# Layer A's dense products by Strassen's seven products over 1024 tokens, with combinations by way of DRAM

## The chip, the cores and the metric

The kernel runs on one core of a Trainium2 chip. The metric is the time of one execution on the device in microseconds (us). TensorE multiplies matrices into PSUM, VectorE (DVE) and ScalarE (ACT) work on PSUM and SBUF, GpSimd (POOL) on SBUF alone; transfers are issued by SyncE (SP) or by POOL, and all of them are carried out by the same 16 DMA engines.

## The reference

2048 tokens of 1024 features go through a layer A (gMLP), then a layer B (attention over a window of 128 tokens with shared keys and values), then a norm. The change touches layer A alone:

```python
def gmlp_mixer(h, w_in, ln_g, ln_b, ws, bs, w_out):     # h = rms_norm(x): 2048 x 1024
    z = h @ w_in                                        # 1024 -> 3 * 2048
    u, v, g = jnp.split(z, 3, axis=-1)
    v = layer_norm(v, ln_g, ln_b)
    v = v.reshape(b, nc, CHUNK, A_GROUPS, A_GROUP_DIM)  # 16 chunks of 128 tokens, 16 groups of 128
    wsm = jnp.where(causal[None], ws, jnp.zeros_like(ws))
    sv = jnp.einsum('gts,bcsgd->bctgd', wsm, v) + bs.T[:, :, None]
    y = u * sv * jax.nn.silu(g)
    return y @ w_out                                    # 2048 -> 1024; x is added to it
```

Everything is float32. The kernel makes a float32 product from three passes: each operand is split into a high part (rounded to the type fp32r) and a low part (the rest), and high x high, high x low and low x high are summed (`mm3`).

## The kernel before, in words

Layer A goes over four blocks of 512 tokens (`NB`, `TB`). For a block:
- `vphase` computes v with tokens on partitions: 4 groups of 512 columns, 4 chunks of tokens, 8 tiles of features: 384 products of 128 x 128 by 128 x 512 (three passes each counted). ACT copies v from PSUM, VectorE takes the statistics (`bn_stats`) and normalizes in place. v stays in SBUF.
- 16 times `proj` for u and `proj` for g (features on partitions, 24 products each: 768 in all), and `gate`: the small product of v with the causal weights, times u, times silu(g) (the last multiplication on POOL), and the split of the result by ACT (high) and VectorE (low).
- `outproj_a`: 8 output tiles of 48 products (384), x added, the result stored to DRAM (`hD`) with its sum of squares.

Weights are a stream: `order` is the list of tiles (1024 columns), `fetch` loads the next by SP's queue and splits it on ACT and VectorE (`split`, L112 and L113), and `weights` keeps three tiles ready (`LOOKAHEAD`); four buffers hold them. Work that fits between products is hung on a count of half pieces (12 products): `half` counts, `at` and `after` register it. In this way the norm of the next block (`stat_steps`, `xn_step`) and 18 jobs `prescale_job` run in layer A: a job loads a tile of layer B's weights, multiplies it by the norm's gain and splits it on ACT and POOL, and stores it to DRAM (`wbD`) through POOL's queue. At the start TensorE multiplies raw x by the weights of v (`FIRST_W`), and the norm is applied to the result. SBUF holds 39 general slots of 512 columns (`GEN_BUFS`).

The order of instructions on each engine is set by the framework's planner from the order of the program; waits are by semaphore, and each engine and queue works in order.

## Time and profile before

| | |
|---|---|
| runs | 2269.25, 2267.98, 2269.21 us; median 2269.21 |
| profiled execution, first to last instruction | 2266.6 us |
| its own time beside its span | the runs' median is 2.6 us above the span |
| TensorE busy / loads of its weights | 99% / 85% |
| VectorE / ScalarE / POOL busy | 55% / 39% / 27% |
| moved by DMA | 319.59 MB, mean 141 GB/s |
| last eviction of layer A begins at | 1471.4 us |

How to read the lines: a line of a group has the source line, the engine, the operation, what it writes and reads, the shape, the count, then the busy time in us and the mean of one in ns, then the idle time of the engine ahead of it and who ended it. A line of the timeline has the start and the duration in us. Matmuls are pipelined, so the distance between two starts, not the duration of one, is the price of a product. In slices a digit is the busy share of one fortieth of the span in tenths.

### The profile page before, as it was taken

Reading aid. Unit: us, or ns where it says so; the run is one execution under the profiler, and the core shown is the slowest. Engines: PE = TensorE matmul, PEld = TensorE weight load, DVE = VectorE, ACT = ScalarE, POOL = GpSimd, SP = SyncE. Lnnn points to the kernel's source line nnn. Section 1 sums busy time; section 2 is a strip of 40 time slices with the busy share of each in tenths; the row PEclk is TensorE's granted clock in tenths of the full one; section 3 lists DMA queues with packets and bytes.
Section 4 is the critical chain, followed back from the end, with each engine's and each line's share of the span. In section 5 each row is a group of like instructions: output and inputs, shape, how many; then the busy total and the mean of one; then the engine's idle time right before and its main releaser. Section 6 shows DMA issues by size and latency. Waiting matters only on the chain.

```text
span 2266.6 us, 31103 instructions
## 1 busy us (share of the span) xinstructions
PE 2239.9 (99%) x11868; PEld 1922.9 (85%) x11868; DVE 1240.9 (55%) x2145; ACT 889.2 (39%) x1781; POOL 619.3 (27%) x667
## 2 busy tenths in 40 slices
PE   8999999999999999999999999999999999999997
PEld 7888888888888888888888888899889889989987
DVE  6543553354453344345335335258957867895785
ACT  5323332323332322323222223135725744662573
POOL 2034322023532003311101111225513622551461
PEclk9999999999999999999999999999999999999999
DMA  6245453335455324325332224543364255336322
GB/s 214 85 154 189 163 204 126 100 120 176 151 202 178 105 93 149 122 92 177 121 107 89 89 93 149 179 174 114 101 219 155 94 195 186 112 121 235 120 94 93
DMA packets 90005, 319.59 MB, mean 141 GB/s; under 512 B 10625, under 2 KB 12929, under 8 KB 78081
## 3 DMA queue, kind: packets, MB, share of 16 engines
q1 hardware_dynamic: 71424, 204.35, 26.8%
q0 software_dynamic: 18432, 113.26, 14.5%
q8 instruction: 94, 1.54, 0.3%
q14 instruction: 55, 0.44, 0.1%
HBM read 280.86 MB, written 36.70 MB: 140 GB/s over the span
## 4 chain that ended last, share of the span: by engine, by line
PE 85%; DVE 6%; issue 3%; ACT 2%; DMA 2%; POOL 2%; POOLq 0%; SPq 0%; DVEq 0%; ACTq 0%
PE ps L116 26%; PE ps L117 26%; PE ps L118 25%; PE ps L375 2%; PE ps L641 2%; PE ps L588 1%; PE ps L619 1%; PE ps L589 1%; DVE w L113 1%; PE ps L560 1%; DVE x_lo L113 1%; DMA s<-h 1%; ACT w L112 1%; DMA s<-in_xT 1%; POOL s L381 0%
## 5 line engine op out<-in xcount | busy, mean ns | idle before, releaser
L113 DVE TENSOR_TENSOR w<-w_raw,w 128x1024 fp32r<-128x1024 f32 x288 | 378.4, 1314 | 369.5 <-ACT w L112 369.1
L116 PE MATMUL ps<-x_hi,w 128*128 128x512 f32 x1280 | 506.3, 396 | 0.0
L117 PE MATMUL ps<-x_lo,w 128*128 128x512 f32 x1280 | 499.0, 390 | 0.0
L118 PE MATMUL ps<-x_hi,w 128*128 128x512 f32 x1280 | 498.6, 390 | 0.0
L112 ACT CAST w<-w_raw 128x1024 fp32r<-128x1024 f32 x288 | 301.0, 1046 | 499.2 <-PE ps L118 375.8
L116 PE MATMUL ps<-w,x_hi 128*128 128x256 f32 (+1 forms) x1024 | 332.1, 324 | 0.0
L118 PE MATMUL ps<-w,x_lo 128*128 128x256 f32 (+1 forms) x1024 | 330.5, 323 | 0.0
L117 PE MATMUL ps<-w,x_hi 128*128 128x256 f32 (+1 forms) x1024 | 330.4, 323 | 0.0
L116 PE MATMUL ps<-s,w 128*128 128x512 f32 (+1 forms) x800 | 305.2, 383 | 4.5 <-ACT s L112 4.5
L117 PE MATMUL ps<-s,w 128*128 128x512 f32 (+1 forms) x800 | 305.0, 381 | 0.1
L118 PE MATMUL ps<-s,w 128*128 128x512 f32 (+1 forms) x800 | 304.4, 381 | 0.0
L118 PEld LDWEIGHTS ps<-x_hi,w 128*128 128x128 f32 x1280 | 240.3, 188 | 50.5
L116 PEld LDWEIGHTS ps<-x_hi,w 128*128 128x128 f32 x1280 | 240.7, 188 | 46.0
L117 PEld LDWEIGHTS ps<-x_lo,w 128*128 128x128 f32 x1280 | 240.8, 188 | 45.7
L627 POOL TENSOR_SCALAR_AFFINE_SELECT s<-s 128x512 fp32r<-128x512 f32 x256 | 184.8, 749 | 101.7 <-ACT s L621 69.3
L117 PEld LDWEIGHTS ps<-w,x_hi 128*128 128x128 f32 x1024 | 194.7, 190 | 15.6
L116 PEld LDWEIGHTS ps<-w,x_hi 128*128 128x128 f32 x1024 | 194.6, 190 | 15.5
L118 PEld LDWEIGHTS ps<-w,x_lo 128*128 128x128 f32 x1024 | 194.7, 190 | 15.1
L381 POOL TENSOR_TENSOR s<-s 128x512 f32<-128x512 f32 x64 | 82.2, 1284 | 396.0 <-DVE s L380 335.6
L116 PEld LDWEIGHTS ps<-s,w 128*128 128x128 f32 x800 | 150.2, 188 | 33.8 <-ACT s L112 6.0
L117 PEld LDWEIGHTS ps<-s,w 128*128 128x128 f32 x800 | 150.5, 188 | 29.2 <-DVE s L113 1.4
L118 PEld LDWEIGHTS ps<-s,w 128*128 128x128 f32 x800 | 150.4, 188 | 28.5
(145 smaller groups left out, 2871.5 us busy)
## 6 DMA issues: line engine op xcount, KB each, us to landing
w<-wb POOLq DMA_DIRECT2D x72, 1024.0 KB, 5.4
w_raw<-in_wug SPq DMA_DIRECT2D x128, 512.0 KB, 3.7
w_raw<-in_wv SPq DMA_DIRECT2D x64, 512.0 KB, 3.7
w_raw<-in_wao SPq DMA_DIRECT2D x64, 512.0 KB, 3.8
s<-in_xT SPq DMA_DIRECT2D x88, 256.0 KB, 4.4
wb<-phl POOLq DMA_DIRECT2D x18, 1024.0 KB, 5.2
w_raw<-in_wbo SPq DMA_DIRECT2D x32, 512.0 KB, 3.8
s<-h SPq DMA_DIRECT2D x64, 256.0 KB, 4.7
```

The source lines that it names most:

```text
L112: A.copy(hi, src)
L113: (lo_eng or V).tensor_tensor(lo, src, hi.bitcast(F32), ALU.subtract)
L116: PE.matmul(ps, ah, bh, start=first, stop=False)
L117: PE.matmul(ps, ah, bl, start=False, stop=False)
L118: PE.matmul(ps, al, bh, start=False, stop=last)
L375: PE.matmul(psm[:, t * P:(t + 1) * P], vt[t][j // 4][:, (j % 4) * P:(j % 4 + 1) * P], ws_sb[:, j, :], start=True, stop=True)
L381: last[0] = G.tensor_tensor(sv, sv, sg, ALU.mult).ins
L560: PE.transpose(pst[:, h * P:(h + 1) * P], sts[t2][:, h].rearrange("p s d -> p (s d)"), ident_r)
L588: PE.matmul(o, lq, kst[:, kv, 0, band, :], start=True, stop=False)
L589: PE.matmul(o, lq, kst[:, kv, 1, band, :], start=False, stop=True)
L627: G.affine_select(out=y.rearrange("p (h q) -> p h q", h=4), in_=x.rearrange("p (h q) -> p h q", h=4), pattern=[[0, 4], [sign, P]], base=ba ...
L641: PE.matmul(po[:, par * 256:(par + 1) * 256], w, x[:, par * 256:(par + 1) * 256], start=n == 0, stop=n == 3)
```

## The change

Layer A goes over two halves of 1024 tokens. Every dense product is seen as 2 x 2 blocks on each side (two halves of the contracted features; two halves of the tokens; two of the output columns, for u and g the columns of u and those of g) and done with seven products of blocks in the form of Winograd, in the order `STEPS`. `chain_of` runs the seven and combines their results: partial sums accumulate in PSUM, others are copied out by ACT (or added to the residual by VectorE) and added later by VectorE. A product of blocks has 4 feature tiles and 12 passes per bank.

- The input side. The seven combinations of x (`combos`: four additions) are split into high and low and stay in SBUF (`X`, 14 tiles of 2048 columns). For the first half VectorE makes them ahead of and during the first v stage (`start_block`, `third`, `fourth`); the norm of x is now applied before the products. For the second half POOL makes them during the first out stage (`x_steps`), the split goes to DRAM (`put_dram` with two buffers `hl`, `setD`), and `load_set` brings it back. The combinations of y take the same way (`ug_pair`, `finish_pair`), as two sets for the two halves of y's features.
- The weight side. `fetch_a` builds the four combined tiles of each weight set on POOL in the first half, from quarters loaded by SP, and stores them (`sumD`); in the second half they are loaded. A weight tile has 512 columns. LOOKAHEAD stays 3, so three tiles are three times 12 products.
- v goes to DRAM (`vD`) through POOL's queue and comes back by groups (`load_v`), and is normalized then (`mix`). The causal weights and their constants take the same way (`wscD`).
- The residual is loaded, and partial and final results of the out stage stored, through POOL's queue (`out_pair`, `pD`, `hD`).
- The prescale jobs are cut into 36 halves, 18 in each out stage.
- General slots: 19 in layer A, 39 in layer B from a pool of its own.

The core of the diff:

```diff
+STEPS = ("11", "12", "s2", "s1", "s3", "s4", "22")
...
+    def fetch_a(n, quarters, sums, make):
...
+        if si is None:
+            raw = rd(qr(n))
+        elif not make:
+            raw = rd(sums[si])
+        elif n == "s2":
+            r21, r22, raw = rd(qr("21")), rd(qr("22")), rd(qr("11"))
+            G.tensor_tensor(r21, r21, r22, ALU.add)
+            G.tensor_tensor(raw, r21, raw, ALU.subtract)
+            G.dma_start(sums[0], r21)
+            G.dma_start(sums[1], raw)
+            kept[key] = r21
...
+        w = wraw[0].tile([P, 1024], F32R, name="wa", bufs=W_BUFS)
+        split(w[:, :512], w[:, 512:], raw)
...
+        def load_set(key, n):
+            new_set(n)
+            for z in range(2):
+                G.dma_start(X[n][z].rearrange("p (k t) -> p k t", k=4), setD[key][n][:, :, z, :].bitcast(F32R))
+
+        def combos(q11, q12, q21, q22, eng):
+            yield q11
+            yield q21
+            t1 = slot()
+            eng.tensor_tensor(t1, q12, q11, ALU.subtract)
+            eng.tensor_tensor(q11, q22, t1, ALU.subtract)
+            yield q11
+            yield t1
+            eng.tensor_tensor(q12, q22, q12, ALU.subtract)
+            yield q12
+            yield q22
+            eng.tensor_tensor(q21, q21, q11, ALU.subtract)
+            yield q21
+
+        def put_dram(key, n, k, t):
+            hl = hltile()
+            split(hl[:, :TB], hl[:, TB:], t)
+            G.dma_start(setD[key][n][:, k], hl.rearrange("p (z t) -> p z t", z=2).bitcast(F32))
...
+        def chain_of(width, product, keep, done, on_step):
+            a = [bank() for _ in range(width)]
+            product(a, "11", True)
+            p1 = keep(a, 11)
+            on_step(0)
+            c = [bank() for _ in range(width)]
+            product(c, "12", True)
+            done(11, c, p1)
+            on_step(1)
+            product(a, "s2", False)
+            u2 = keep(a, 12)
+            on_step(2)
+            c = [bank() for _ in range(width)]
+            product(c, "s1", True)
+            p5 = keep(c, 22)
+            on_step(3)
+            product(a, "s3", False)
+            done(22, a, p5)
+            on_step(4)
+            product(c, "s4", False)
+            done(12, c, u2)
+            on_step(5)
+            product(a, "22", False)
+            done(21, a, None)
+            on_step(6)
...
+        def by_columns(banks, n, first):
+            xh, xl = X[n]
+            for ps in banks:
+                wh, wl = weights()
+                for k in range(4):
+                    cs, ts = slice(k * P, (k + 1) * P), slice(k * TB, (k + 1) * TB)
+                    mm3c(ps, wh[:, cs], wl[:, cs], xh[:, ts], xl[:, ts], first and k == 0)
+                half()
...
+        for sb in range(2):
+            ln = vphase(sb)
             pend = None
+            for kh in range(2):
+                for jj in range(4):
+                    pend = ug_pair(sb, kh, jj, ln, pend, ("Y0_", sb) if kh == 1 and jj == 3 else None)
+            acc = [None, None]
+            if sb == 0:
+                for k in range(4):
+                    for i, f in enumerate(x_steps(k)):
+                        after(4 + 8 * k + i, f)
+            for i in range(18):
+                after(6 + 2 * i, lambda i=i, sb=sb: prescale(18 * sb + i))
+            finish_pair(pend, ln)
+            for kh in range(2):
+                for m in range(2):
+                    nxt = None
+                    if m == 1:
+                        nxt = ("Y1_", sb) if kh == 0 else ("X", 1) if sb == 0 else None
...
+                    out_pair(sb, kh, m, acc, nxt)
```

More of the change, by code (lines that the diff above doesn't have):

```diff
@@ L107, in trunk @@
     g_sb = glob.tile([P, 4, KD], F32, name="g_sb")
[L108 removed]
+    nc.sync.dma_start(g_sb, gains)
     a_g, kv_g, b_g, f_g = (g_sb[:, i, :] for i in range(4))
@@ new lines, in xn, with put, second @@
+        def xn(h, k):
+            V.scalar_tensor_tensor(xq[h, k], xq[h, k], a_g[:, k:k + 1], rbox[h], ALU.mult, ALU.mult)
+        def put(n, k, t):
+            ks = slice(k * TB, (k + 1) * TB)
+            split(X[n][0][:, ks], X[n][1][:, ks], t)
+        start_block(0, 0, 0)
+        while events:
+            half()
+        for k in range(4):
+            xn(0, k)
+            put("11", k, xq[0, k])
+        h0 = now[0]
+        for k in range(4):
+            def second(k=k):
+                xn(0, k + 4)
+                put("12", k, xq[0, k + 4])
+            at(h0 + 1 + k // 2, second)
```

478 lines of the change are left out of this document (297 added, 181 removed).

## The prediction

> **What bounds the kernel now.** I read the page first (busy shares, slices, transfer rate), then the timeline of TensorE, then the groups of instructions by line, then short windows for the transfers.
>
> ```profile
> span 2266.6 us, 31103 instructions
> ...
> PE 2239.9 (99%) x11868; PEld 1922.9 (85%) x11868; DVE 1240.9 (55%) x2145; ACT 889.2 (39%) x1781; POOL 619.3 (27%) x667
> ...
> PE   8999999999999999999999999999999999999997
> ...
> DVE  6543553354453344345335335258957867895785
> ...
> POOL 2034322023532003311101111225513622551461
> ...
> GB/s 214 85 154 189 163 204 126 100 120 176 151 202 178 105 93 149 122 92 177 121 107 89 89 93 149 179 174 114 101 219 155 94 195 186 112 121 235 120 94 93
> ```
>
> TensorE never pauses; POOL and the transfers have room in every slice of layer A (slices 1 to 26). The timeline of TensorE gives the price of one product and shows that nothing stands between products:
>
> ```profile
> 6.76 1.22 PE L116 MATMUL ps<-w,s 128*128 128x512 f32 x2 [6.76 <-ACT w L112]
> ...
> 117.22 0.39 PE L118 MATMUL ps<-x_hi,w 128*128 128x512 f32 x1
> 117.45 1.05 PE L375 MATMUL ps<-ws_sb,s 128*128 128x128 f32 x8
> 118.25 0.48 PE L116 MATMUL ps<-x_hi,w 128*128 128x512 f32 x1
> ...
> 1439.64 0.39 PE L118 MATMUL ps<-s,w 128*128 128x512 f32 x1
> ...
> 1469.78 0.39 PE L116 MATMUL ps<-s,w 128*128 128x512 f32 x1
> ```
>
> From 1439.64 to 1469.78 lie 133 starts: 0.2266 us each. A gate's small products add about 0.9 us. Layer A of before has 4 blocks x (384 + 768 + 384) = 6144 wide products: 1392 us, with 64 gates at 0.9 (58 us), the first start at 6.8 and some small change to the last eviction of the layer, which begins at 1471.4 (row below). So layer A is TensorE's own rate, and layer B takes the remaining 795 us, unchanged in kind.
>
> ```profile
> L400 DVE TENSOR_TENSOR s<-ps,s x32: 682/692/692, 304.9 to 1471.4; 128x512 f32<-128x512 f32 x32
> ```
>
> **What the change removes.** Seven products for eight: 6144 x 7/8 = 5376, 768 fewer, 768 x 0.2266 = **-174 us** on TensorE, the full gain. Gates: 16 x 2 x 4 small products per 1024 tokens, as many as before. What it adds lies on the other engines and the queues; their prices:
>
> ```profile
> L381 POOL TENSOR_TENSOR s<-s 128x512 f32<-128x512 f32 x64 | 82.2, 1284 | 396.0 <-DVE s L380 335.6 <-issue 60.4
> ...
> L378 DVE SCALAR_TENSOR_TENSOR s<-ps,lngb_sb,cb 128x512 f32<-128x512 f32 x64 | 48.0, 750 | 176.6 <-PE ps L375 176.6
> ...
> L112 ACT CAST s<-s 128x512 fp32r<-128x512 f32 x75 | 46.6, 621 | 282.0 <-POOL s L381 257.3 <-POOL s L184 22.4 <-DVE s L184 2.3
> ...
> L113 DVE TENSOR_TENSOR s<-s 128x512 fp32r<-128x512 f32 x64 | 44.3, 693 | 149.5 <-ACT s L112 149.5
> ...
> L113 POOL TENSOR_TENSOR phl<-pw,phl 128x1024 fp32r<-128x1024 f32 x18 | 43.2, 2400 | 16.2 <-ACT phl L112 16.2
> ...
> L330 POOL TENSOR_TENSOR pw<-pw,g_sb 128x1024 f32<-128x1024 f32 x18 | 34.1, 1892 | 73.9 <-DMA pw<-in_wqg 65.7 <-DMA pw<-in_wkv 8.3
> ...
> L299 DVE SCALAR_TENSOR_TENSOR s<-s,g_sb 128x512 f32<-128x512 f32 x32 | 25.2, 816 | 15.2 <-DMA s<-in_xT 14.8 <-DVE s L299 0.3
> ...
> L401 POOL DMA_DIRECT2D h<-s x32 | 17.9, 558 | 248.4 <-DVE s L400 248.4
> ...
> L184 DVE TENSOR_TENSOR s<-s 128x512 f32<-128x512 f32 x24 | 16.6, 691 | 14.7 <-ACT s L181 14.7
> ...
> L196 POOL TENSOR_TENSOR r<-m,neghalf 128x4 f32<-128x4 f32 x11 | 11.4, 1037 | 54.3 <-DVE m L194 54.2
> ...
> L193 DVE TENSOR_REDUCE m<-s 128x4 f32<-128x512 f32 x11 | 7.5, 683 | 0.2
> ```
>
> So a 512-wide POOL operation costs 1.28 us, a transfer issued from POOL 0.56 us of POOL, a 512-wide VectorE operation 0.69 us. For the transfers, two windows in which they ran at a full share:
>
> ```profile
> core 0: us, PE busy (x) PEld busy (x) DVE busy (x) ACT busy (x) POOL busy (x), PEclk, DMA share, GB/s
> 4.00:8.00 4.00, 1.22 (x2) 0.50 (x2) 2.01 (x3) 1.76 (x2) 0.00 (x0) 1.00 0.99 387
> 8.00:12.00 4.00, 3.98 (x10) 2.88 (x11) 1.61 (x3) 2.05 (x3) 0.00 (x0) 1.00 1.04 406
> ```
>
> I take 390 GB/s as all that the transfers can move. Each half of the new layer A (1024 tokens) has three stages: v (56 weight tiles of 12 products, 152 us of TensorE), u and g (8 pairs of 168 products and four gates, 38.1 + 3.6 = 41.7 us each, 333 us), out (4 pairs, 152 us). I go stage by stage and add what each takes above TensorE's time.
>
> **Start: +33.** Before, TensorE began on raw x at 6.8. Now the first product needs the norm: 8 tiles of x and 3 of weights (2.9 MB at 390 GB/s from 2 us on, 9.4 us), then one after another square, add, split (ACT 0.62, POOL 1.28), mean, reduce, power (1.04), back through TensorE, multiply, split: about 12 us. First product at about 22: +15. The first four steps (11, 12, s2, s1) take TensorE 10.9 us each, and VectorE must have made s2 by 22 + 30 = 52: 16 scalings (13), 16 splits of x (11), 12 splits of weights (8), 8 square adds and a second norm (9), 8 combinations (6), 8 operations on the first quarter (6), 53 us from 21 on: s2 complete at 74 instead of 52, of which I take +18 (3 to 22, as TensorE works while the tiles come). Bounds of the term +20 to +45.
>
> **u and g, first half: +10.** A pair has two weight sets to build: per set 4 POOL adds and 4 stores of the sums. POOL per pair: 8 adds + 4 combinations of y + 4 gates = 16 x 1.28 = 20.5, and 8 + 7 + 4 transfers x 0.56 = 10.6: 31 of 41.7 us. VectorE: 14 + 7 splits, 4 x 0.75 gate, 4 multiplies, 6 evictions, 16 short scalings: about 28. Bytes: per set 10 reads and 4 writes of 0.262 MB, y 3.7 MB, v and its constants 1.3 MB: 12.3 MB, 32 us. All three fit, none by much, and the lookahead is three tiles of 2.7 us where it was three of 5.4. A wait of POOL for VectorE's split stands ahead of the weight sums on POOL's queue, and TensorE is three tiles away from these. Between 0 and +54 (second rival); I take +10, nearest to the bound in which the sums fit.
>
> **Out, first half: +138.** Here everything meets: 8 weight sets are built, residuals come and go through POOL's queue, half of the prescale jobs and all combinations of x for the second half are placed here, and Y1 and X are loaded. POOL: 32 weight adds, 20 combinations, 4 gates, 14 square adds, 2 norm splits: 72 x 1.28 = 92; 18 half prescale jobs at 0.95 + 1.20 = 39; transfers: 32 sums, 32 residual loads, 32 stores, 36 of prescale, 52 of x, 28 of sets, 9 others = 221 x 0.56 = 124. **Sum 255 us against 152 of TensorE.** Bytes: weights 29.4, residuals 16.8, prescale 14.2, x 21, two sets 29.4, y 3.7: 114 MB, at 390 GB/s **290 us**. TensorE needs the weight sums, the residuals and the sets, all of which stand in the same queue in about the order of the program, so it can run only a few tiles ahead. What covered such work before was POOL at 27%; that cover is gone here. I take the transfers' 290: 290 - 152 = +138. Bounds: if the prescale work alone slides into the next stage (39 + 36 x 0.56 = 59 of POOL's 255) +44; if handoffs of POOL and the two buffers of the split combinations cost a tenth more, 330, +178.
> The Trainium skill, DMA: Bandwidth & Descriptors, section Specifications, gives about 358 GB/s as the limit from HBM for one core. By it the stage would be 114/0.358 = 318 us and the sum 28 us more; the windows above moved 387 and 406, so here the trace disagrees and I stay with it.
>
> **v, second half: +3; u and g, second half: +2.** The sums are read, not made: POOL has 32 stores in the one, 8 operations and 11 issues (16.4 us) per pair in the other, VectorE as above without the x work. Up to +10 and +5, for the load of X and short of nothing below zero.
>
> **Out, second half: +22.** POOL: 8 + 14 + 2 operations (31), prescale 39, 121 issues (68): 138 of 152. Bytes: weights 14.7, residuals 16.8, prescale 14.2, Y1 14.7, the late part of Y0 some 10, the rest 6: 76 MB, 195 us; part of it runs in the last pair of u and g, so half of the 43 is taken (0 to +45).
>
> **Layer B: +2.** Same work; its slots now come free only when layer A's pool closes (0 to +10).
>
> **Sum:** -174 + 33 + 10 + 138 + 3 + 2 + 22 + 2 = **+36**. The profiled span is 2266.6, 2.6 us below the median 2269.2 of the runs; both move alike, so 2269 + 36 = **2305 us**.
>
> **Rivals.**
> 1. *POOL lets the late work go by* (ends faster). Place: the prescale jobs and stores of the first out stage, which nothing in layer A reads, slide into the second v stage, where POOL has 32 issues in 152 us; the transfers slide with them, and the sets of X stream into the v stage, whose steps last 10.9 us. Then the stage costs about +50 and the second out stage +15: -174 + 33 + 5 + 50 + 3 + 2 + 15 + 2 = -64, **2205**. It decides from 36 us of slid work on. For it: the row of slices shows POOL at 0 to 3 tenths where it has no due work. Against: the jobs stand earlier in the program than the sums that TensorE waits for.
> 2. *VectorE and POOL shut each other out* (slower still). In the prescale work of before:
>
> ```profile
> 537.34 1.23 DVE L113 TENSOR_TENSOR w<-w_raw,w 128x1024 fp32r<-128x1024 f32 x1 [1.73 <-ACT w L112]
> ...
> 541.91 2.40 POOL L113 TENSOR_TENSOR phl<-pw,phl 128x1024 fp32r<-128x1024 f32 x1 [1.16 <-ACT phl L112]
> ...
> 542.82 2.58 DVE L113 TENSOR_TENSOR w<-w_raw,w 128x1024 fp32r<-128x1024 f32 x1
> ```
> The same split takes VectorE 1.23 us at 537.34 and 2.58 at 542.82, where it ends 1.09 us after POOL's operation (541.91 + 2.40): it waited for it. If every such pair excludes the other, POOL's chain in a u/g pair becomes 20.5 + 10.6 and 25 VectorE operations with two inputs in SBUF x 0.69 (17.2) = 48.3 against 41.7: 8 x 6.6 = +53 instead of +10; in the out stage 255 + 107 x 0.69 = 329 instead of 290, 39 more: **2387**. For it: the three rows. Against: it needs each one to be hit. The Trainium skill, SBUF — State Buffer, section Who interferes with whom, states the same: a VectorE instruction with two SBUF inputs contends with a GpSimd one that reads SBUF, and the second blocks; the rows agree.
> 3. *All of it is hidden*: issues from POOL turn out to cost TensorE nothing and only the start remains: -174 + 33 + 6 = -135, **2134**. Against: 255 us of POOL in a stage of 152.
> 4. *The products don't fall*: excluded by the count, 5376 for 6144; TensorE's records of layer A would show it.
>
> **How the numbers follow.** Forecast 0.50 (own range 2250 to 2370), rival 1 0.27, rival 2 0.13, rival 3 0.10. Faster: rivals 1 and 3 and the lowest edge of the forecast, 0.39; within 0.2% (4.5 us, what a measurement of this kernel can tell) 0.04; slower 0.57. Range 2180 to 2400: it leaves out rival 3 and the upper part of rival 2.
>
> **What would show it.** In the profile after: first product at about 22 us; TensorE's slices at 9 in u/g and v, and at 4 to 6 for a stretch of some 290 us that begins near 550 us; in it POOL at 8 or 9 tenths and over 350 GB/s; waits of TensorE for weight splits that wait for POOL or for a transfer. Wrong would be: no such stretch (rivals 1 and 3), or one already from 200 us on (rival 2).

## The result, and the profile after

The changed kernel takes **2638.72 us** (median of four runs, 2633.39 to 2648.25) against 2269.06 for the kernel before (four runs, 2267.98 to 2269.25): ratio 1.1636, 95% interval 1.1613 to 1.1659. The forecast was 2305 with a range to 2400: the sign was right, the size was not; +370 us where +36 was forecast. The page of the changed kernel, in the order of the lines shown of before:

```profile
span 2631.7 us, 33230 instructions
...
PE 2202.0 (84%) x11100; PEld 1836.3 (70%) x11100; DVE 1645.3 (63%) x2847; ACT 972.6 (37%) x2151; POOL 1248.0 (47%) x1552
...
PE   4788988879553357899999996748899999999998
...
POOL 2675555665567577211344445554243253253352
PEclk8999999989776678899999998879999999999999
...
GB/s 164 227 257 230 214 233 229 230 218 300 332 269 299 337 257 340 201 172 144 178 198 210 203 319 311 295 270 244 134 113 184 163 111 184 175 100 183 188 94 88
```

TensorE's matmuls fell from 11868 to 11100, by 768: the products were saved as forecast. But TensorE's row, 9 from the second slice on before, now shows 3 to 8 in most of slices 1 to 16 and again in slices 25 to 27, and the granted clock falls with it. So the question is what each stage takes above its products. Its boundaries are read from TensorE's timeline, at the turn from the last products and gates of one stage to the first products of the next, to some 5 us; the windows between them (length; busy time and count of TensorE, its weight loads, VectorE, ScalarE, GpSimd; granted clock, share of the DMA engines, GB/s):

```profile
core 0: us, PE busy (x) PEld busy (x) DVE busy (x) ACT busy (x) POOL busy (x), PEclk, DMA share, GB/s
24.00:248.00 224.00, 182.07 (x690) 138.08 (x691) 148.23 (x230) 79.24 (x143) 127.81 (x169) 0.91 0.63 212
248.00:671.00 423.00, 363.68 (x1598) 293.94 (x1598) 294.81 (x405) 135.59 (x245) 247.35 (x269) 0.92 0.71 242
671.00:1046.00 375.00, 191.28 (x677) 144.68 (x676) 143.13 (x166) 71.71 (x122) 254.56 (x323) 0.73 0.88 301
1046.00:1218.00 172.00, 162.82 (x683) 129.99 (x682) 78.75 (x130) 54.88 (x93) 31.82 (x50) 0.96 0.58 189
1218.00:1562.00 344.00, 339.63 (x1592) 280.62 (x1590) 252.41 (x396) 135.15 (x243) 129.07 (x143) 1.00 0.62 207
1562.00:1823.00 261.00, 179.19 (x680) 141.08 (x681) 112.52 (x144) 57.97 (x98) 141.85 (x183) 0.82 0.88 291
1823.00:2632.00 809.00, 780.37 (x5184) 706.78 (x5182) 602.29 (x1357) 427.63 (x1192) 310.71 (x410) 0.99 0.42 144
```

In this order: v, u/g and out of the first half, the same of the second half, layer B. Above TensorE's need (152, 333, 152 us, by the prediction's working), and with the start at 24 us instead of 6.8:

| term | forecast | measured |
|---|---|---|
| start and v, first half | +33 | +89 (17 + 72) |
| u/g, first half | +10 | +90 |
| out, first half | +138 | +223 |
| v, second half | +3 | +20 |
| u/g, second half | +2 | +11 |
| out, second half | +22 | +109 |
| layer B | +2 | +12 (809 against 797 from the last product start of layer A) |
| products | -174 | -174 |

The terms add up to +380; 13 of it stood in layer A of before as well (its last product started at 1469.8, its products and gates make 1457), which leaves 367 for the 365 between the two spans.

Two bills of the prediction came out: GpSimd's busy time in the first out stage (forecast 255 us, row 254.56) and the bytes of the out stages (forecast 114 and 76 MB; 301 GB/s x 375 us = 113, 291 x 261 = 76). That the first agrees to the digit is luck: its parts were 92 us for 92 (additions and the like), 42 for 39 (prescale) and 133 for 124 (issues), and they overlap by 12. So the work was counted rightly; what failed is the time that this work takes, and where TensorE waits for it. The waits in the first out stage (engine, waiting instruction, releaser: us in all, times, longest):

```profile
PEld ps L126 <- ACT wa L116: 165.8, 15, 48.8
...
ACT hl L116 <- POOL s L439: 87.5, 12, 16.0
DVE hl L117 <- ACT hl L116: 86.2, 21, 13.8
DVE s L606 <- DMA s<-p: 49.7, 10, 14.3
...
POOL s L439 <- DMA s<-in_wqg: 31.5, 10, 9.9
```

TensorE waits for ScalarE's casts of the weights, and ScalarE is busy 72 of 375 us there. It waits itself: each engine takes its instructions in order, and at the head of ScalarE's queue stands the cast of a prescaled tile (made at L439), with weight casts behind it. GpSimd, which makes that tile, stands at its head for the tile's load. One such chain in the timelines of ScalarE, of GpSimd and of TensorE (start, duration; in brackets the idle time before and what ended it):

```profile
910.22 0.62 ACT L116 CAST hl<-s 128x512 fp32r<-128x512 f32 x1 [5.16 <-DMA wb<-hl]
926.28 0.62 ACT L116 CAST hl<-s 128x512 fp32r<-128x512 f32 x1 [15.44 <-POOL s L439]
927.50 0.62 ACT L116 CAST wa<-w_raw 128x512 fp32r<-128x512 f32 x1 [0.60 <-POOL w_raw L214]
```
```profile
912.40 0.55 POOL L437 DMA_DIRECT2D s<-in_wqg  x1
...
914.03 1.27 POOL L213 TENSOR_TENSOR w_raw<-w_raw 128x512 f32<-128x512 f32 x1
925.21 1.04 POOL L439 TENSOR_TENSOR s<-s,g_sb 128x512 f32<-128x512 f32 x1 [9.91 <-DMA s<-in_wqg]
926.20 1.27 POOL L214 TENSOR_TENSOR w_raw<-w_raw 128x512 f32<-128x512 f32 x1
```
```profile
928.17 0.80 PE L126 MATMUL ps<-xh,wa 128*128 128x512 f32 x1 [48.40 <-ACT wa L116]
...
933.06 0.63 PE L126 MATMUL ps<-xh,wa 128*128 128x512 f32 x1
933.49 0.63 PE L127 MATMUL ps<-xl,wa 128*128 128x512 f32 x1
...
938.17 0.39 PE L127 MATMUL ps<-xl,wa 128*128 128x512 f32 x1
938.40 0.39 PE L128 MATMUL ps<-xh,wa 128*128 128x512 f32 x1
```

GpSimd issues the load of a tile that nothing in layer A needs at 912.40, multiplies it at 925.21 and only then makes the weight sum of L214 (926.20); the cast of that sum follows at 927.50, the product at 928.17, after 48 us in which TensorE had nothing. In 34 of these 48 us ScalarE stood for prescale jobs: 13.57 ahead of its cast at 903.92, then 5.16 (for one of the two buffers of the split) and 15.44. And TensorE restarts slowly: products start 0.43 us apart until 933.9, 0.23 from 937.2 on.

### The profile page after: what moved, and what is told of

Same layout as the page of the kernel before. It is cut to its first block, busy times and chain, and to the rows that moved or that the text cites. A ratio compares the mean times of both kernels' runs of the same rounds, so it can differ in the third digit from the quotient of the medians.

```text
span 2631.7 us, 33230 instructions
## 1 busy us (share of the span) xinstructions
PE 2202.0 (84%) x11100; PEld 1836.3 (70%) x11100; DVE 1645.3 (63%) x2847; ACT 972.6 (37%) x2151; POOL 1248.0 (47%) x1552
## 4 chain that ended last, share of the span: by engine, by line
PE 43%; DMA 17%; POOL 11%; DVE 10%; issue 8%; ACT 2%; SPq 0%; POOLq 0%; DVEq 0%; ACTq 0%
PE ps L128 7%; PE ps L126 7%; PE ps L127 7%; PE ps L120 6%; PE ps L122 5%; PE ps L121 5%; DMA w_raw<-in_wug 3%; DMA s<-in_wqg 3%; DMA s<-in_xT 2%; DMA Y_s<-hl 2%; PE ps L909 1%; DMA s<-p 1%; DMA vp<-v 1%; DVE wa L117 1%; DVE vp L534 1%
## 5 line engine op out<-in xcount | busy, mean ns | idle before, releaser
L126 PE MATMUL ps<-xh,wa 128*128 128x512 f32 x1344 | 563.1, 419 | 270.1 <-ACT wa L116 180.8
L128 PE MATMUL ps<-xh,wa 128*128 128x512 f32 x1344 | 556.4, 414 | 50.7 <-DVE wa L117 50.5
L117 DVE TENSOR_TENSOR wa<-w_raw,wa 128x512 fp32r<-128x512 f32 x448 | 386.2, 875 | 292.4 <-ACT wa L116 291.4
L127 PE MATMUL ps<-xl,wa 128*128 128x512 f32 x1344 | 551.3, 410 | 0.0
L126 PEld LDWEIGHTS ps<-xh,wa 128*128 128x128 f32 x1344 | 269.8, 201 | 342.4 <-ACT wa L116 205.6
L116 ACT CAST wa<-w_raw 128x512 fp32r<-128x512 f32 x448 | 273.3, 619 | 401.5 <-PE ps L128 308.5
L128 PEld LDWEIGHTS ps<-xh,wa 128*128 128x128 f32 x1344 | 267.4, 199 | 127.6 <-DVE wa L117 65.8
L127 PEld LDWEIGHTS ps<-xl,wa 128*128 128x128 f32 x1344 | 269.4, 200 | 60.2
L126 PE MATMUL ps<-wa,xh 128*128 128x512 f32 x448 | 183.7, 412 | 17.8 <-ACT s L476 6.4
L127 PE MATMUL ps<-wa,xh 128*128 128x512 f32 x448 | 183.9, 411 | 4.7 <-DVE wa L117 4.7
L120 PE MATMUL ps<-w,hn 128*128 128x256 f32 x640 | 184.1, 288 | 0.0
L121 PE MATMUL ps<-w,hn 128*128 128x256 f32 x640 | 182.3, 285 | 0.0
L122 PE MATMUL ps<-w,hn 128*128 128x256 f32 x640 | 182.2, 285 | 0.0
L128 PE MATMUL ps<-wa,xl 128*128 128x512 f32 x448 | 181.9, 407 | 0.1
L534 DVE TENSOR_SCALAR vp<-vp,mv,rs 128x128 f32<-128x128 f32 x256 | 149.3, 655 | 14.5 <-DMA vp<-v 11.0
```

Source lines behind the costliest of these rows:

```text
L116: A.copy(hi, src)
L117: (lo_eng or V).tensor_tensor(lo, src, hi.bitcast(F32), ALU.subtract)
L120: PE.matmul(ps, ah, bh, start=first, stop=False)
L121: PE.matmul(ps, ah, bl, start=False, stop=False)
L122: PE.matmul(ps, al, bh, start=False, stop=last)
L126: PE.matmul(ps, ah, bh, start=first, stop=False, skip_group_check=True)
```

## The experiments

All are edits of the changed kernel; where not said otherwise each is one run with its profile. e2, e4, e5, e9, e10, e13 and e17 leave out part of the work, the others do all of it. The four runs of the changed kernel lie within 15 us of each other, and a stage that an edit leaves alone comes out within some 5 us (v of the first half takes 223 to 226 in e1, e4, e5 and e7, v of the second 170 to 175 in e8 to e13); smaller differences say nothing. Their stages in us (v, u/g, out of the first half; v, u/g, out of the second), from TensorE's timelines:

| kernel | time | v | u/g | out | v | u/g | out |
|---|---|---|---|---|---|---|---|
| changed kernel | 2638.7 | 224 | 423 | 375 | 172 | 345 | 261 |
| e1 prescale moved | 2539.9 | 225 | 421 | 298 | 171 | 396 | 192 |
| e2 no sums | 2481.1 | 192 | 346 | 329 | 175 | 342 | 259 |
| e3 issued later | 2582.8 | 228 | 414 | 364 | 170 | 342 | 231 |
| e4 quarter sets | 2528.5 | 223 | 413 | 336 | 159 | 338 | 225 |
| e5 = e1 + e4 | 2450.4 | 223 | 419 | 249 | 163 | 392 | 165 |
| e6 sums on VectorE | 2611.1 | 219 | 409 | 371 | 174 | 344 | 260 |
| e7 = e3 + prescale moved | 2505.7 | 226 | 412 | 297 | 201 | 344 | 190 |
| e8 longer lead | 2617.6 | 221 | 405 | 373 | 170 | 342 | 256 |
| e9 no stores of sums | 2585.6 | 219 | 404 | 357 | 170 | 344 | 254 |
| e10 no additions | 2581.2 | 206 | 395 | 367 | 173 | 346 | 259 |
| e11 nine raw buffers | 2639.7 | 224 | 431 | 376 | 170 | 344 | 260 |
| e12 casts on VectorE | 2646.3 | 229 | 417 | 385 | 170 | 349 | 262 |
| e13 loads only | 2489.5 | 193 | 352 | 336 | 175 | 343 | 256 |
| e14 gate and y on VectorE | 2617.6 | 231 | 410 | 376 | 169 | 335 | 263 |
| e15 gate on VectorE | 2623.9 | 233 | 414 | 377 | 170 | 335 | 259 |
| e16 = e7 + e14 | 2503.9 | 225 | 413 | 300 | 206 | 337 | 187 |
| e17 sums on VectorE, no stores | 2546.2 | 200 | 380 | 355 | 174 | 343 | 258 |
| e18 = e7 + e6 + later stores | 2509.6 | 219 | 409 | 300 | 210 | 343 | 191 |

**The out stages: bytes, or waits at the heads of the queues?** The theory of the prediction (T1: bytes; the rate was too high) stood against a rival (T2: waits at the heads, as in the chain above).

*e1: the prescale jobs leave the out stages.*
```diff
+            if sb:
+                for i in range(36):
+                    after(8 + 4 * i, lambda i=i: prescale(i))
-            for i in range(18):
-                after(6 + 2 * i, lambda i=i, sb=sb: prescale(18 * sb + i))
```


> The 36 half prescale jobs leave the two out stages and are spread over the v and u/g stages of the second half; the work is the same. Theory T1 (the transfers' throughput sets the out stages; at a full share they move about 330 GB/s here): each out stage loses 14.2 MB, 43 us, so the whole is 2640 - 86 = about 2550 us, and the second half's v and u/g stages stay as they are. Theory T2 (engines and queues work in order and stand at their heads waiting for something that was issued too late, POOL for the load of its own prescale job and ScalarE for POOL's result): each out stage loses some 100 us, the whole is about 2440 us.

*e4: a quarter of the bytes of each set of combinations is loaded.*
```diff
-            new_set(n)
-                G.dma_start(X[n][z].rearrange("p (k t) -> p k t", k=4), setD[key][n][:, :, z, :].bitcast(F32R))
+                G.dma_start(X[n][z][:, :TB], setD[key][n][:, 0, z, :].bitcast(F32R))
```


> Leaves out three quarters of the bytes of each load of a set of x or y (the first 512 of 2048 columns come in, the rest keeps older values); the number of loads, of products and of everything else stays. 11 MB less for each of the five sets. T1: the first out stage (the late part of Y0, Y1 and X) loses up to 33 MB, 100 us, the second 22 MB, 67 us: about 2470 us. T2: only what waits for these loads themselves, up to 40 us: about 2600 us.

*e5: both edits.*


> The move of the prescale jobs (alone 2540 us) and the quarter loads of the sets (alone 2529 us) together; leaves out three quarters of the bytes of each set load. With the prescale jobs gone the first out stage took 298 us and moved about 340 GB/s. T1 (bytes bind there now): 25 MB less bring it to about 240 us and the second out stage from 192 to about 165: in all about 2450 us. T2 (waits at the heads of POOL and ScalarE bind it still): only what the quarter loads save outside the out stages, some 20 us: about 2515 us.

*e3: use further from load. The combinations are stored one step later, and a prescale job is cut into load, multiplication three steps later, split and store five steps later.*
```diff
-            G.tensor_tensor(w3, w3, g[...], ALU.mult)
-            hl = hltile()
-            ...
+            after(3, second)
+            after(5, third)
...
-                        if s == 2:
+                        if s == 3:
```


> Same work and same bytes, but each step is issued later than what it waits for: a prescale job's multiplication three half pieces (8 us) after its load and its split two later; the combinations of y and x one step ahead of their splits. T1: nothing changes, 2625 to 2645 us. T2: the waits of POOL for prescale loads (99 us in the trace) and most of those of ScalarE for POOL ahead of its casts go: about 2500 us.

The windows of the out stages: both of e1, both of e4, then both of e5.

```profile
670.00:968.00 298.00, 181.75 (x679) 140.69 (x679) 136.99 (x166) 60.95 (x104) 191.85 (x254) 0.79 0.99 336
1535.00:1727.00 192.00, 168.66 (x694) 136.17 (x695) 103.74 (x146) 49.33 (x81) 81.20 (x114) 0.91 0.96 325
```
```profile
660.00:996.00 336.00, 188.78 (x689) 144.53 (x688) 142.99 (x171) 74.10 (x127) 247.62 (x324) 0.76 0.81 277
1493.00:1718.00 225.00, 179.82 (x704) 142.28 (x703) 111.67 (x137) 59.39 (x102) 137.14 (x178) 0.87 0.77 257
```
```profile
667.00:916.00 249.00, 177.85 (x705) 138.70 (x704) 139.59 (x171) 63.68 (x109) 184.48 (x253) 0.86 0.90 315
```
```profile
1472.00:1637.00 165.00, 159.85 (x702) 130.39 (x701) 100.67 (x136) 50.55 (x84) 72.44 (x106) 0.99 0.78 264
```

With the prescale jobs gone (e1) the DMA engines are busy 0.99 and 0.96 of the stage and move 336 and 325 GB/s: what is left is a matter of bytes, 100 MB in 298 us, and fewer bytes then help further (e5: 249 and 165, where bytes were expected to give 240 and 165). With the prescale jobs in place (e4), fewer bytes save 39 and 36 us too, but leave the engines at 0.81 and 0.77: there something else holds the stage as well. TensorE's waits for the weight casts in the first out stage, 165.8 us in the changed kernel, are 122.9 in e4 and 42.9 in e1:

```profile
PEld ps L126 <- ACT wa L116: 122.9, 11, 36.2
```
```profile
PEld ps L126 <- ACT wa L116: 42.9, 6, 24.9
```

In e1 the profile names no releaser ("issue") for another 61.3 us of such waits, the most of any there; the longest pause of TensorE among them, 31.8 us up to 870.7, lies in a stretch (838 to 871) in which the DMA engines were at a full share (1.04) and moved 347 GB/s.

So both theories hold in part, and their savings nearly add up (77 and 39 us apart and 126 together in the first out stage, 69 and 36 apart and 96 together in the second): at a full share these stages move 325 to 342 GB/s (e1, e7), not 390, and something more puts an estimated 35 to 40 us on top in the first out stage (375 against 113 MB at 336 GB/s, 336 us). That this is the waits at the heads is read from the chain above and from the casts' waits; e1 also takes 63 us of GpSimd's work out of the stage, and e3, which changes no work but puts distance between load and use, gets 11 us of it in the first stage and 30 in the second (364 and 231). The total of e1, 2540, is where T1 had it (2550), but by luck: the out stages lost 77 and 69 us where bytes gave 43 each, and the moved work is not free: the second u/g stage grew from 345 to 396, with ScalarE waiting 95.5 us for the prescaled tiles there.

*e7: e3 with the prescale jobs moved into the second half's v and u/g stages, at shorter steps.*
```diff
+                    after(4 + 3 * i // 2, lambda i=i: prescale(i))
```


> The 36 half prescale jobs lie close together at the start of the second half, in its v stage, each with its multiplication three half pieces after its load and its split two later, and the combinations of y and x one step ahead of their splits. The u/g stage of the second half, which took 396 us with half of the jobs in it, goes back to 345; out stages 290 and 180: about 2455 us if the v stage keeps its 171 us (POOL has some 120 us of work for the jobs there); up to 2510 if the two buffers for splits hold the jobs up.

2505.7: the u/g stage keeps its 344, out keeps what e1 won (297 and 190), and v of the second half pays 30 (201).

**The u/g stage of the first half: 423 us for 333 of products.** Here the transfers are at 0.71 of their time, so bytes alone don't explain it. What is new is that weight sums are made and stored. The waits in that stage:

```profile
ACT hl L116 <- POOL s L543: 130.9, 14, 12.3
POOL w_raw L213 <- DMA w_raw<-in_wug: 58.1, 13, 7.0
...
PE ps L128 <- DVE wa L117: 32.6, 8, 5.6
...
PE ps L126 <- ACT wa L116: 21.7, 6, 5.3
```

TensorE waits for the splits of the weights, ScalarE for the gate products of GpSimd (L543), and GpSimd for loads of weights that it is to add.

*e2: no sums; every combined weight is a plain quarter.*
```diff
+        raw = rd(quarters[PLAIN.index(n) if n in PLAIN else 0])
```
(in place of the loads, additions and stores in `fetch_a`)


> Leaves out the combined weight tiles: each of the four combined tiles of a set is one plain quarter, loaded like the others, in both halves; no additions of weights on POOL, no stores of sums. 128 POOL additions, 128 issues from POOL and 59 MB less, all in the first half. T1: the first out stage loses 15 MB, 45 us, the u/g stage of the first half, which isn't bound by bytes, some 40: about 2550 us. T2: POOL no longer stands waiting for weight loads ahead of the gates, so the first u/g stage comes down to its 333 us of products plus little (-70), the first v stage by 30 and the out stage by 60: about 2480 us.

*e6: the additions on VectorE.*
```diff
-            G.tensor_tensor(r21, r21, r22, ALU.add)
+            V.tensor_tensor(r21, r21, r22, ALU.add)
```
(the other three alike)


> The combined weight tiles of the first half are added on VectorE instead of POOL, with the same loads and stores. If the first u/g stage (423 us for 333 us of products) is held by POOL's own time and by POOL and VectorE shutting each other out: it comes down to about 350 us, the first out stage by 30, the first v stage, where VectorE is full, grows by 15: about 2550 us. If it is held by weight loads that arrive late, VectorE now stands at its head in POOL's place: 415 to 440 us, and 2620 to 2660 us in all.

*e8: weights further ahead.*
```diff
-W_BUFS = 4
-LOOKAHEAD = 3
-GEN_A = 19
+W_BUFS = 5
+LOOKAHEAD = 4
+GEN_A = 17
```


> Weight tiles are made ready four ahead instead of three, with five buffers instead of four; the general slots of layer A are 17 instead of 19 to make room. If the pauses of the first u/g stage come from a lead (three tiles of 2.7 us) that is shorter than the lateness of a tile: 423 goes to about 390 us and the whole to about 2590. If a late tile is late by more than a tile's time (the engines' order is what holds it): less than 10 us, 2630 to 2650.

e2 takes 346 there, nearly the products' time, and 192 in the first v: the sums hold both stages, 77 and 32 us. But neither GpSimd's time for them (e6: 409) nor the lead of the casts (e8: 405) gives back more than 14 and 18 of the 77. In e6 VectorE stands 72 us for these loads in GpSimd's place. In e8 the split tiles do come earlier: TensorE waits 13.6 us for them, not 54.3. In their place it waits 29.5 us for copies out of PSUM (L476) by ScalarE, which still stands 138.3 us for gate products: something else now stands behind the same head. In the first out stage e2 saves 46 us, with the bytes, additions and stores of the sums gone. The chain as the timeline of ScalarE and that of GpSimd show it:

```profile
343.91 0.62 ACT L116 CAST wa<-w_raw 128x512 fp32r<-128x512 f32 x1
355.01 0.62 ACT L116 CAST hl<-s 128x512 fp32r<-128x512 f32 x1 [10.48 <-POOL s L543]
355.54 1.14 ACT L116 CAST wa<-w_raw 128x512 fp32r<-128x512 f32 x2
```
```profile
346.32 1.38 POOL L222 TENSOR_TENSOR w_raw<-w_raw 128x512 f32<-128x512 f32 x1 [1.95 <-DMA w_raw<-in_wug]
...
350.64 1.26 POOL L222 TENSOR_TENSOR w_raw<-w_raw 128x512 f32<-128x512 f32 x1 [2.10 <-DMA w_raw<-in_wug]
...
353.67 1.30 POOL L543 TENSOR_TENSOR s<-s 128x512 f32<-128x512 f32 x1
```

GpSimd stands for a load of weights (346.32, 350.64), so the gate product (353.67) is late, so ScalarE stands 10.48 us at the cast of y with two weight casts behind it. Four theories were put to the next runs: stores (S), additions (A), loads and raw buffers (R), ScalarE's wait for the gate (G).

*e9: sums made, not stored* (the four `G.dma_start(sums[...])` gone; the reloads, one a set in the first half and four in the second, take plain quarters; a set's four stores are 256 packets of 4 KB in the trace, where the text below counts 2048 of 512 bytes).


> Leaves out the four stores of the weight sums in each set of the first half (2048 packets of 512 bytes a set); the three loads that read them back take a plain quarter, so loads, additions and products stay as many. The question is what holds the u/g stage of the first half, 423 us in the changed kernel, 346 without loads, sums and stores together, 333 by its products. Theory S (the stores' bytes, their issue on POOL and the reload behind them hold it): 350 to 370, the run about 2575. Theory R (the two more loads of each set and the seven raw buffers hold it): 405 or more, the run 2615 to 2640. Theory G (ScalarE standing for POOL's gate products, with the weight casts behind it): about 400, the run 2610.

*e10: the four additions gone.*


> Leaves out the four additions of each weight set on POOL in the first half (32 sets, 128 additions of 512 columns); all loads and stores stay. Theory A (the chain load, addition, addition, cast comes too late for the products): u/g of the first half 350 to 370, the run about 2560. Theory R (the extra loads and the raw buffers): 405 or more, v of the first half gains 10 at most, the run 2610 or more. Theory G (ScalarE waits for POOL's gate products because POOL is held by the additions and by their loads): 360 to 380, the run about 2580.

*e11: more raw buffers.*
```diff
-GEN_A = 19
-RAW_A = 7
+GEN_A = 17
+RAW_A = 9
```


> Nine raw weight buffers instead of seven, and 17 general buffers instead of 19 to make the room; nothing else. Theory R (the queue of loads stands for a free raw buffer, 171 us in the u/g stage of the first half, and that is what the products wait for in the end): u/g of the first half 370 to 390, the run about 2590. Theories S, A and G: within 8 us of 423 there; the out stages may lose up to 10 us by the two buffers, the run 2630 to 2650.

*e12: the high casts of the combinations on VectorE.*
```diff
-            split(hl[:, :TB], hl[:, TB:], t)
+            V.tensor_copy(hl[:, :TB], t)
+            V.tensor_tensor(hl[:, TB:], t, hl[:, :TB].bitcast(F32), ALU.subtract)
```


> The high cast of the combinations of x and y, of 512 columns, is made by VectorE instead of ScalarE; nothing left out. It takes from the head of ScalarE's queue the cast that waits for POOL: 207 us in all behind the gate products, 147 us behind the prescale and residual tiles, with weight casts behind both. Theory G (these waits delay the weight casts): u/g of the first half 375 to 395, out of the first half 340 to 355, the run about 2570. Theories S, A and R: VectorE takes the wait over with the low halves of the weights behind it, u/g within 8 us of 423, the run 2630 to 2660.

404, 395, 431, 417: none of the four alone holds it. e11 says that two more raw buffers, at the price of two general ones, win nothing (431), e12 that VectorE takes over part of ScalarE's wait (48.7 us for the gate), with splits of weights behind it (TensorE waits 46.4 us for VectorE's low halves and 3.1 for ScalarE's casts, 32.6 and 21.7 in the changed kernel). In e9 and in e10 GpSimd still waits for the loads of weights, before an addition in the one and before a store in the other, and longer than in the changed kernel (122 and 130 us for 92), though the stage is shorter: how long it stands is not by itself what the stage loses. The next theory, L: any such wait keeps GpSimd's whole queue.

*e13: neither additions nor stores; the loads stay.*


> Leaves out the four additions and the four stores of each weight set in the first half and loads plain quarters instead of the stored sums; the loads stay as many as in the changed kernel, and no instruction of GpSimd waits for one of them. Theory R (the extra loads and the raw buffers hold the u/g stage of the first half): 400 or more there, the run 2560 to 2600. Theory L (the loop of queues, with GpSimd's wait for a load of weights as its link): 345 to 360 there, the run about 2500. If the parts only add up, as each took its own share (19 for the stores, 28 for the additions): 376, the run about 2540.

*e14: gate products and combinations of y on VectorE; e15: the gate products alone.*
```diff
-                G.tensor_tensor(us[h], us[h], sgs[h], ALU.mult)
+                V.tensor_tensor(us[h], us[h], sgs[h], ALU.mult)
...
-                            gens.append(combos(u[0][0], u[0][1], u[1][0], u[1][1], G))
+                            gens.append(combos(u[0][0], u[0][1], u[1][0], u[1][1], V))
```
(e15 has the first pair of lines only)


> The gate products and the combinations of y are made by VectorE instead of GpSimd; nothing left out. ScalarE's casts of y then wait for nothing that stands behind a load of weights. Theory L: u/g of the first half 350 to 375 (VectorE has 44 us more there: 8 pairs of 8 instructions at 0.69), the run about 2580. Theory R: 405 or more, the run 2615 to 2640. Against both: VectorE, 294 us busy there, is itself the next bound, and the second half's u/g stage, 344, grows by up to 20.

> Only the gate products go to VectorE; the combinations of y stay on GpSimd, so the four plain quarters' casts are free of GpSimd and the combined ones are not; nothing left out. Theory L: half way, 380 to 400 in the u/g stage of the first half, the run about 2610. Theory R: 415 or more, the run 2630 to 2645.

*e16: e14's edit in e7.*


> The version with the prescale in the second half's v and u/g stages and the longer distance from load to use, and with it the gate products and the combinations of y on VectorE; nothing left out. Theory L: 45 to 65 less than without the move, 2440 to 2460. Theory R: 2495 to 2520. In neither does it come near the kernel before, 2269: the bytes of the two out stages alone hold 85 us more than their products, and the v stage of the second half keeps its 30.

e13 takes 352, with the transfers at the same 0.71 and 237 GB/s:

```profile
216.00:569.00 353.00, 341.93 (x1592) 279.89 (x1592) 255.06 (x397) 136.39 (x245) 131.70 (x145) 1.00 0.71 237
```

So the extra loads hold next to nothing (352 for e2's 346): the stage is lengthened by the additions and stores that wait for them, and by both more than by each (71 us without both, 28 and 19 without one). (A reserve: buffers that nobody reads come free when their load lands; that this alone made the difference is made unlikely by e11, not excluded.) But e14 takes 410, not 350 to 375, and e15 414, not 380 to 400: the gate is not the one link. (Both are about what theory R expected, but against R stands e13.) Waits of e14 in that stage:

```profile
ACT hl L116 <- DVE s L543: 86.6, 14, 11.8
POOL Y_s L372 <- DVE hl L117: 86.4, 10, 12.8
DVE vp L534 <- DMA vp<-v: 66.4, 13, 8.9
...
POOL w_raw L213 <- DMA w_raw<-in_wug: 47.3, 15, 7.5
```

ScalarE still stands for the gate, now VectorE's, and VectorE stands 66 us for v, whose load is issued by GpSimd, behind the same weight sums. e16 (2503.9) is the fastest complete version, but not told apart from e7 (2505.7).

*e17: additions on VectorE and no stores, so that GpSimd waits for no weights.*


> The four additions of each weight set run on VectorE, and their stores are left out (three later loads take a plain quarter instead), so no instruction of GpSimd waits for a load of weights; VectorE stands for these loads in its place. Theory Q (GpSimd's queue is the link, by whatever it has to issue): u/g of the first half 350 to 370, the run 2510 to 2530. Theory P (each part takes a share of its own: 14 for the additions moved to VectorE, 19 for the stores): 385 to 395, the run about 2560. Theory H (any queue that stands for a late load of weights is as bad, VectorE's too): 395 or more.

*e18: e7 with the additions on VectorE and each store issued two weight tiles later.*
```diff
+        def late(dst, src):
+            after(2, lambda: G.dma_start(dst, src))
-            G.dma_start(sums[0], r21)
+            late(sums[0], r21)
```
(the other three alike)


> On the version with the prescale in the second half's v and u/g stages and the longer distance from load to use (2506, 412 in the u/g stage of the first half): the additions on VectorE, and each store of a sum issued two weight tiles later, when the sum should be there, so that GpSimd does not stand for it; nothing left out. Theory Q: u/g of the first half 360 to 380, the run about 2460. Theory P: about 395, the run about 2490. Theory H, or stores that GpSimd still stands for because the loads are later than two tiles: 400 to 410, the run about 2500.

e17: 380, between theory Q (350 to 370) and P (385 to 395). Against e13's 352, 28 us remain although GpSimd waits for no weights: VectorE stands for them now, 53 us in all, and is busy 33 us longer (288 for 255). Against e6's 409, taking the stores off GpSimd's queue gave 29, where the same stores gave 19 beside additions on GpSimd (e9). e18 gave nothing, 409 for e7's 412: two tiles later the sum was still not there, and GpSimd stood at the stores as before, by its waits in that stage:

```profile
POOL su L205 <- DVE w_raw L225: 52.9, 15, 4.7
DVE w_raw L225 <- DMA w_raw<-in_wug: 41.2, 16, 4.0
```

What this settles: of the 77 us between e2 and the changed kernel the extra loads take 6 (e13 against e2). The other 71 come with the instructions that wait for these loads: 28 with the additions on VectorE and no stores (e17 against e13), 43 more with additions and stores on GpSimd (423 against 380). As far as the traces go they are TensorE's pauses for split weights and for v, and the slow restarts behind them: its pauses in that stage are 59 us in the changed kernel, 27 in e17 and 11 in e13. What stays argued: that the standing in line costs this, and not the work of the additions and stores. For it speaks that the engines have room (GpSimd busy 247 and VectorE 295 of 423 us, transfers at 0.71); but no run kept the work and took the waits away, and e18, which was to do so, did not. What stays open too: how the 43 divide among the things queued behind GpSimd (gate products, loads of v and of sets, stores of combinations), since taking away one left the others; what a longer lead would give together with gate products that ScalarE doesn't stand for, which was not tried; and why the loads themselves come late with seven buffers as with nine.

## Why the prediction was wrong, point by point

The step that failed in most of the terms: the prediction takes the largest of the sums of each engine and of the transfers as a stage's time, or concludes that a stage in which all of them fit is hidden. The sums of work were nearly right; the rate of the transfers was not, and the waits between the queues had no price.

- **Products, -174: right.** 768 matmuls fewer in the records.
- **Out, first half, +138 for +223.** The work was right (255 us of GpSimd, 114 MB); the step that failed is "I take 390 GB/s as all that the transfers can move". That came from two 4-us windows of loads alone; over a stage with loads and stores the engines at a share of 0.99 moved 336 (e1). 113 MB at 336 make 336 us, +184: 46 of the missing 85. The rest, 39, is by subtraction; the prediction had the handoffs as an upper bound ("a tenth more, 330") on too low a base (and a tenth on its 290 is 319, not 330): a tenth on 336 is 370, and 375 was measured. The Trainium skill, DMA: Bandwidth & Descriptors, section Specifications (about 358 GB/s from HBM for one core), would have given 318, and was set aside for those windows; the stages of e1 moved less than either (336 and 325 GB/s). Why the mix runs slower than the loads of the start was not tried.
- **Out, second half, +22 for +109.** The step that failed is "half of the 43 is taken" as part of the transfers would run in the u/g stage before: all 76 MB moved inside the stage (291 x 261). At 325 GB/s they need 234 us, +82. The other 27 are by subtraction; moving the prescale takes more than its bytes away (e1: 192). TensorE's pauses there are mostly (56 of 81 us) for VectorE's additions to the residual, whose loads GpSimd issues in the same queue in which it stands 58 us for loads of prescale tiles.
- **u/g, first half, +10 for +90.** The step that failed is to add up each engine's work (31 us of GpSimd, 28 of VectorE, 32 of transfers in a pair of 41.7) and to conclude that it fits. It does fit: GpSimd was busy 247 of 423 us. What had no price is that each wait at a head stops all behind it (59 us of pauses of TensorE, for splits and for v). "A wait of POOL for VectorE's split stands ahead of the weight sums" named one direction of it; the one that mattered ran the other way, the sums' wait for their loads ahead of gates, loads and stores. Its upper bound, +54, came from the lock between VectorE and GpSimd and was passed.
- **Start and v, first half, +33 for +89.** The first product came at 24.4, forecast 22. The v stage took 72 above its products, forecast +18: 32 of these go with the sums (e2: 192), for which the prediction had priced VectorE's splits of the weights only; the other 40 stay also without sums. Some 22 of them stand in the first three steps (24.8 to 79.8 in e2, where the products need 32.7; 24.4 to 86.7 in the changed kernel). There the prediction gave VectorE until 22 + 30 = 52 for s2, though by its own 10.9 us a step s2, the third, was due at 44. The rest no run here takes apart.
- **v, second half, +3 for +20.** 13 go with the bytes of the X sets (e4: 159). **u/g, second half, +2 for +11, layer B +2 for +12**: not taken apart.
- **The clock.** No term allowed for it: behind most pauses TensorE restarts at half pace. In layer A 373 product starts lie 0.38 to 0.7 us apart, 316 of them at 0.43, instead of 0.227: together 82 us of the 380, spread over the terms above (29 in the first out stage, 19 in the first u/g stage).
- **Rivals.** 1 (late work slides by) and 3 (all hidden) didn't come; 2 was nearest in time (2387) but the runs speak against its reason: VectorE's splits do get longer beside GpSimd's additions (a weight tile's 930 ns in the mean in that stage, 775 in e6 with the additions off GpSimd, 754 in e2), but in e6, where that is gone, the stage keeps 409 of 423 us.
- **Signs named in advance.** TensorE at 4 to 6 tenths over a stretch: it came (slices 11 to 16 at 5, 5, 3, 3, 5 and 7), later than 550 and longer than 290 us; 8 or 9 tenths of GpSimd and over 350 GB/s in it did not (5 to 7 tenths, 340 at most), which fits waits in line better than one full resource.

Could the change be mended? The lowest time that any run reached for each stage, the incomplete kernels' too, sums to 23 + 192 + 346 + 249 + 159 + 335 + 165 + 809 = 2278 us against a span of 2266.6 before. No run points to a version that beats the kernel before; the best complete one is at 2503.9.

## What to carry to other kernels

A stage in which each engine's work fits is not yet hidden: list, for each in-order queue, the instructions that wait for a transfer, and what stands behind them; a tile that nobody needs soon (the prescale) does harm there, and belongs where the queue has little else to do (e7: 30 us more in a v stage, 78 and 71 less in the out stages, part of it by e3's distance from load to use). A price for transfers has to come from a stretch with the same mix of loads and stores, at a full share over a whole stage, not from a few microseconds of loads. Moving one waiting instruction to another engine mostly moved the wait here (e6, e12, e14); getting these loads to land much earlier, which no run here did, would be the thing to try first.

## What the runs showed of the hardware

- After a pause TensorE's 128x512 products start 0.43 us apart mostly for 2 to 5 us and then 0.23 (rows at 933 and 938; 37 such stretches of five starts or more in layer A, 33 of them within 10 us behind a pause of 2.7 us or more, the other four behind 2.0 to 2.5); the granted clock was 0.73 over the first out stage. The Trainium skill, TensorE: Matmul & The Clock Gate, section What's actually happening, gives a half-rate clock after an idle window of about 3.4 us; the trace agrees in the half rate (0.43 for 0.227), but the four stretches behind 2.0 to 2.5 us began after less.
- The price of issuing a transfer from GpSimd is not 0.56 us whatever its shape: 128 runs of 4 KB cost 0.545, 512 runs of 2 KB 0.766, 1024 runs of 512 bytes 0.911. Rows of the groups (count, busy us, mean ns, idle before):

```profile
L372 POOL DMA_DIRECT2D Y_s<-hl x64 | 34.8, 545 | 113.7 <-DVE hl L117 110.3 <-DVE s L615 1.8 <-DVE vp L534 1.3
...
L526 POOL DMA_DIRECT2D vp<-v x32 | 29.2, 911 | 99.0 <-PE ps L538 78.1 <-DVE s L540 9.8 <-DMA v<-s 7.8
...
L352 POOL DMA_DIRECT2D xh<-Y_s x16 | 12.3, 766 | 0.9 <-DMA X<-hl 0.9
```
